# Buffer reuse, the order of one projection, early products and piecewise loads in a transformer block

## The chip, the cores and the metric

The kernel runs on one core of one Trainium2 chip. The metric is the device time of one execution in microseconds (us), as the median of several runs. One execution was also taken with the hardware profiler; all stretches below are microseconds from the start of that execution's span.

## The reference

One decoder block in float32 for 512 tokens of width 2048. A normalized input goes through one wide projection into a query latent and a key-value latent (512 each), a rotary key (64), the halves u and v of a gating unit (1024 each) and two gates (2048 each). Two branches follow, latent attention with 16 heads and a causal gating unit; their outputs are projected, gated and added, projected again by w_out and added to x. Then comes a SwiGLU feed-forward network (FFN, width 5632) and a last norm:

```python
D_MODEL, SEQ, D_FF = 2048, 512, 5632
q_lat, kv_lat, k_pe, u, v, g0, g1 = split(rms_norm(x) @ w_in)
a = mla(q_lat, kv_lat, k_pe) @ w_o_attn        # 16 heads, causal
s = (gelu(u) * (tril(w_s) @ rms_norm(gelu(v)) + b_s)) @ w_o_sgu
x = x + (sigmoid(g0) * a + sigmoid(g1) * s) @ w_out
h = rms_norm(x)
x = x + (silu(h @ w_gate) * (h @ w_up)) @ w_down
return rms_norm(x, g_final)
```

## The kernel before

**Arithmetic.** Each float32 operand is split into a high and a low part, and each matmul is done as three matmuls on the parts (`mm3`, L167 to L169). A weight chunk (`chunk`, 512 KB) is loaded by a DMA on SP's queue (L151) into a float32 buffer, cast to its high part on ACT (L152), and the low part is made by a subtraction on DVE (L153); 24 matmuls of 512 columns use it. The wide projections for u and the gates ("the x run"), and for gate and up of the FFN, go by `run` instead: each job loads 2 MB of weights (L408), makes seven sums of its quarters (L374 cast, L375 subtraction, L394 and L397 sums), and multiplies each with one of seven "forms" of the activations. One such product is 24 matmuls of 256 columns (L385 to L387), three for each of eight pairs (kp) of operand blocks. `forms_x` and `f_forms` make the forms of one kp (a cast at L331 and a subtraction at L117).

**Memory.** Nearly all of SBUF is two arenas with an allocator: `ar` (144 units of 1 KB per partition) holds split operands, `af` (52 units) holds raw float32 loads and results. `get` takes the free piece of least cost: pieces of 4 units prefer the part of `ar` from unit 112 up, then a block of eight units that is already partly in use ("packing"), and only then the piece that has been free for longest. The program's order on each engine is fixed when the program is built; a new tile waits for the last reader of the piece it is given.

**Order of stages.** The latents (w_lat) to 100 us; the v projection in two passes (g = 0, 1) of four PSUM banks each, 108 to 217 us, with 32 transposes of the latents (`latents`, L311) and the making of x's forms between its chunks; the x run to 646 us; attention and the gating unit to 957 us; w_osgu, w_oattn and w_out to 1477 us, the latter in four column blocks c with `scaled(c - 1)` (16 transposes, L810) inside the next one; the FFN's products, 1497 to 2391 us, which begin with `f_rest` (the last transposes, L810, the forms of kp 6 and 7, and `row_bcast`, L214 and L215); and the down projection to 3041 us. In the down projection, `down` multiplies eight hidden tiles (four kp) with four column blocks of w_down, five times over, 80 chunks in all; the next eight tiles are loaded on POOL's queue (L159) and split (L135 on ACT, L136 on DVE) by `hidden` before it. Four last hidden tiles have their weights prepared apart (L926). PE's order follows the code.

Of the kernel before, what the change touches and what calls it, by code (L numbers as in the profile page):

```python
# [9 lines left out]
F32 = mybir.dt.float32  # L10
# [35 lines left out]
class Arena:  # L46

    def __init__(self, tile, units, keep, large):  # L50
        self.tile, self.keep, self.large, self.clock = tile, keep, large, 0
        self.free_at = [0] * units
        self.held = {}

    def get(self, n, low=False):
        best = None
        end = (self.keep if n >= self.large else 0) or len(self.free_at)
        for i in range(0, end - n + 1, n):
            span = self.free_at[i:i + n]
            if None not in span:  # L60
                block = self.free_at[i // 8 * 8:i // 8 * 8 + 8]
                cost = (i,) if low else (n < self.large and i < self.keep, n < 8 and None not in block, max(span), -i)
                if best is None or cost < best[0]:
                    best = cost, i
# [22 lines left out]
def tile_block(ctx: ExitStack, tc, a):  # L87
# [3 lines left out]
    sml = ctx.enter_context(tc.tile_pool(name="sml", bufs=8))  # L91
    psp = ctx.enter_context(tc.tile_pool(name="psp", bufs=8, space=bass.MemoryType.PSUM))
    drm = ctx.enter_context(tc.tile_pool(name="drm", bufs=1, space=bass.MemoryType.DRAM))
    ar = Arena(cst.tile([P, NR * 256], F32R, name="ar"), NR, NX, 14)
    af = Arena(cst.tile([P, NF * 256], F32, name="af"), NF, 0, 16)

    def T():
        return af.get(2)
# [143 lines left out]
        return ss  # L242


    lat = []
    lacc = cst.tile([P, 2 * NB], F32, name="lacc")

    def lat_out(g, banks):
        row = []
        for tb, ps in enumerate(banks):  # L250
            z = T()
            nc.scalar.activation(junk, ps, AF.Square, scale=rx[:, tb:tb + 1],
                                 accum_out=lacc[:, g * NB + tb:g * NB + tb + 1])
            nc.vector.tensor_scalar(out=z, in0=ps, scalar1=rx[:, tb:tb + 1], scalar2=None, op0=ALU.mult)
            row.append(z)
        lat.append(row)

    lbanks = [[PS() for _ in range(NB)] for _ in range(2)]
    for g in range(2):
        for kp in range(8):  # L260
# [7 lines left out]
    rx = rsqrt(total(xacc, NB, "xs"), D, NB, "rx")  # L268
    lat_out(0, lbanks[0])
    lat_out(1, lbanks[1])  # L270
    rl = rsqrt(lacc, R, 2 * NB, "rl")


    raw = af.get(4)
# [19 lines left out]
        nc.vector.tensor_tensor(out=kp0[own], in0=kps[own], in1=kp0[own], op=ALU.add)  # L294
    nc.vector.tensor_tensor(out=kp0, in0=kp0, in1=rxb, op=ALU.mult)
    store(kped, kp0)
    for g in range(2):
        for tb in range(NB):
            nc.vector.tensor_scalar(out=lat[g][tb], in0=lat[g][tb], scalar1=rl[:, g * NB + tb:g * NB + tb + 1],
                                    scalar2=None, op0=ALU.mult)  # L300


    latd = drm.tile([8, P, 512], F32, name="latd")
    vvd = drm.tile([2, NB, P, 512], F32, name="vvd")
    vacc = cst.tile([P, 2 * NB], F32, name="vacc")

    def latents(g):
        for k in range(4):
            ps = PS()
            for tb in range(NB):  # L310
                nc.tensor.transpose(out=ps[:, tb * P:(tb + 1) * P], in_=lat[g][tb][:, k * P:(k + 1) * P],  # L311
                                    identity=ident)
            v = (V_Q, V_KV)[g] + k
            t = T()
            nc.scalar.activation(t, ps, AF.Copy, scale=vec[:, v:v + 1])
            store(latd[g * 4 + k], t)
        drop(lat[g])

    fx = []

    def forms_x(f, fx):
# [24 lines left out]
        drop(raw)  # L346
        forms_x(f, fx)

    af.keep = 32
    for g in range(2):  # L350
        banks = [PS() for _ in range(NB)]
        for kp in range(8):
            gemm_tm(banks, a["w_v"][g, kp], kp, aT, kp == 0, kp == 7)
            if g == 0 and kp in (2, 4):
                latents(kp // 2 - 1)
            if g == 0 and kp in (3, 5, 7):
                x_forms(kp // 2 - 1)
            if g == 1:
                drop(aT[kp * 2:kp * 2 + 2])
                if kp in (1, 3, 5):  # L360
                    x_forms(kp // 2 + 3)
        for tb, ps in enumerate(banks):
            t = T()
            nc.scalar.activation(t, ps, AF.Gelu_apprx_tanh, scale=rx[:, tb:tb + 1])
# [12 lines left out]

    FORM = (0, 5, 6, 4, 1, 2, 3)

    def product(ps, w, xs, first):  # L380
        hi, lo = w
        for kp, x in enumerate(xs):
# [5 lines left out]
        drop(w)  # L388

    def bank():  # L390
        return PS()[:, :256]
# [10 lines left out]
    class Unit:  # L402
# [32 lines left out]
            drop(self.raw)  # L435
            return w

        def multiply(self, i, w, fx):
            if i == 0:
# [3 lines left out]
            product(self.banks[(0, 1, 2, 1, 0, 1, 2)[i]], w, xs, i < 3)  # L443

        def read(self, i):
            ba, bb, bd = self.banks
# [20 lines left out]
    def run(jobs, fx, rest, ends, lead=3):  # L467


        jobs = list(jobs)  # L470
        last = 7 * len(jobs) - 7
        units, ready = {}, {}

        def unit(n):
            if n < len(jobs):
                units[n] = Unit(*jobs[n])

        unit(0)
        for g in range(last + 7 + lead + 1):
            g1, g2 = g - lead, g - lead - 1  # L480
            if g2 >= 0:
                units[g2 // 7].read(g2 % 7)
            if g < last + 7:
                ready[g] = units[g // 7].weights(g % 7)
                if g % 7 == 6:
                    unit(g // 7 + 2)
            if g == lead - 1:
                rest()
                unit(1)
            if 0 <= g1 < last + 7:  # L490
# [37 lines left out]
        x_forms(7)  # L528

    latT = []  # L530

    def latents_in(g):
        latT.append([move(load(latd[g * 4 + k])) for k in range(4)])

    run(x_jobs(), fx, x_rest, {2: lambda: latents_in(0), 4: lambda: latents_in(1)})
    qnT, kvT = latT
    af.keep = 0


    post = T()  # L540
# [283 lines left out]
    order = {(1, 3): 0, (1, 5): 1, (2, 3): 2, (3, 1): 3, (3, 3): 4, (3, 5): 5}  # L824
    for c in range(4):
        if c == 2:
            af.keep = 32
# [63 lines left out]
    run(ffn_jobs(), ff, f_rest, {2: lambda: hid.extend(hidden(0, 4)), 4: lambda: hid.extend(hidden(4, 4))})  # L891


    af.keep = 0
    for tb in range(NB):
        for c in range(4):
            h[tb][c] = load(hd[tb, :, c * 512:(c + 1) * 512])
# [2 lines left out]
        nc.vector.scalar_tensor_tensor(out=h[tb][c], in0=ps, scalar=rest[:, tb:tb + 1], in1=h[tb][c], op0=ALU.mult,  # L900
                                       op1=ALU.add)

    def down(k0, hid):
        for c in range(4):
            banks = [PS() for _ in range(NB)]
            n = len(hid) // 2
# [6 lines left out]
    k0 = 0  # L913
    while k0 < 40:
        nxt = hidden(k0 + 8, 8 if k0 < 32 else 4)
        down(k0, hid)
        k0 += 8
        hid = nxt


    wd = []
# [115 lines left out]
```

## Time and profile before

| | before |
|---|---|
| median of 3 runs | 3056.25 us (3053.21 to 3058.05) |
| profiled execution | 3052.1 us, span 3050.3 us |
| PE busy | 2761.0 us (91% of the span) |
| DVE busy | 1742.5 us (57%) |
| ACT busy | 1102.3 us (36%) |
| mean granted TensorE clock | 0.956 of full speed |
| DMA | 363.13 MB, mean 119 GB/s |

PE is TensorE, and "granted clock" is the share of full speed that the chip gave it; a stretch is at 1.00 (2.4 GHz) or 0.50 (1.2 GHz), and a value between is a mean over both. A busy time of PE near the length of a stretch says that PE sets its pace there; where it is well below, something else does.

### The profile page before, as it was taken

How to read it: one execution, taken by the hardware profiler on the slowest of the kernel's cores; microseconds unless marked ns; L12 is line 12 of the kernel's file. 1: busy time of each engine (PE TensorE's matmuls, PEld its weight loads, DVE VectorE, ACT ScalarE, POOL GpSimd, SP SyncE). 2: the span in 40 equal slices, each digit the busy share in tenths (PEclk: the TensorE clock that was granted, in tenths of full speed). 3: DMA queues.
4: the chain of work that ended last, by engine and by line, in shares of the span. 5: the costliest groups of instructions: out<-in, count | busy, mean ns of one | idle time of the engine just before them, and what ended most of it. 6: DMA issues, size and time to landing. Idle time of an engine off the chain costs nothing.

```text
span 3050.3 us, 41608 instructions
## 1 busy us (share of the span) xinstructions
PE 2761.0 (91%) x17320; PEld 2481.5 (81%) x17320; DVE 1742.5 (57%) x2194; ACT 1102.3 (36%) x1541; POOL 197.4 (6%) x369
## 2 busy tenths in 40 slices
PE   8888999988997789998799999999999697797896
PEld 7778999977886568887699999999999575575665
DVE  4357777776664334333688778787887332333334
ACT  5244444444563222233434444444434211211113
POOL 1000000011001210000000000000000100000000
PEclk9998999999999899999899999999999798898997
DMA  6332333343223544324233233333333422222223
GB/s 255 121 132 107 135 123 127 139 132 123 99 80 114 162 156 145 125 86 130 96 125 125 102 120 121 122 112 111 125 125 126 130 85 95 90 90 93 87 85 109
DMA packets 103900, 363.13 MB, mean 119 GB/s; under 512 B 14176, under 2 KB 14176, under 8 KB 103712
## 3 DMA queue, kind: packets, MB, share of 16 engines
q1 hardware_dynamic: 72720, 260.60, 24.4%
q0 software_dynamic: 29552, 97.28, 9.4%
q8 instruction: 135, 2.21, 0.3%
q10 hardware_dynamic: 1440, 2.60, 0.2%
q14 instruction: 53, 0.43, 0.0%
HBM read 315.07 MB, written 45.35 MB: 118 GB/s over the span
## 4 chain that ended last, share of the span: by engine, by line
PE 49%; DMA 8%; issue 5%; DVE 3%; ACT 3%; POOL 0%; ACTq 0%; POOLq 0%; SPq 0%; DVEq 0%
PE b L385 9%; PE b L386 9%; PE b L387 9%; PE b L167 8%; PE b L169 7%; PE b L168 7%; DMA af<-in_w_down 5%; DVE ar L153 2%; DMA af<-hidd 2%; ACT ar L152 2%; DMA af<-in_w_out 1%; POOL af L159 0%; ACT ar L135 0%; DVE ar L136 0%; ACT ar L331 0%
## 5 line engine op out<-in xcount | busy, mean ns | idle before, releaser
L385 PE MATMUL b<-ar 128*128 128x256 f32 x3584 | 1018.6, 284 | 20.3 <-ACT ar L331 11.5
L387 PE MATMUL b<-ar 128*128 128x256 f32 x3584 | 1017.6, 284 | 2.5 <-DVE ar L117 2.5
L386 PE MATMUL b<-ar 128*128 128x256 f32 x3584 | 1017.5, 284 | 0.0
L167 PE MATMUL b<-ar 128*128 128x512 f32 (+1 forms) x2016 | 796.2, 395 | 235.6 <-ACT ar L152 147.0
L168 PE MATMUL b<-ar 128*128 128x512 f32 (+1 forms) x2016 | 782.9, 388 | 0.0
L169 PE MATMUL b<-ar 128*128 128x512 f32 (+1 forms) x2016 | 761.9, 389 | 3.8 <-DVE ar L153 2.8
L385 PEld LDWEIGHTS b<-ar 128*128 128x128 f32 x3584 | 691.5, 193 | 21.7 <-ACT ar L331 12.1
L387 PEld LDWEIGHTS b<-ar 128*128 128x128 f32 x3584 | 691.4, 193 | 3.1 <-DVE ar L117 3.1
L386 PEld LDWEIGHTS b<-ar 128*128 128x128 f32 x3584 | 691.6, 193 | 0.0
L375 DVE TENSOR_TENSOR ar<-af,ar 128x1024 fp32r<-128x1024 f32 x448 | 544.4, 1223 | 251.3 <-ACT ar L374 249.8
L167 PEld LDWEIGHTS b<-ar 128*128 128x128 f32 x2016 | 391.1, 194 | 344.9 <-ACT ar L152 168.6
L374 ACT CAST ar<-af 128x1024 fp32r<-128x1024 f32 x448 | 459.5, 1046 | 480.7 <-DVE af L397 371.6
L153 DVE TENSOR_TENSOR ar<-af,ar 128x1024 fp32r<-128x1024 f32 (+1 forms) x224 | 268.5, 1204 | 593.8 <-ACT ar L152 581.7
L152 ACT CAST ar<-af 128x1024 fp32r<-128x1024 f32 (+1 forms) x224 | 230.6, 1034 | 721.9 <-DMA af<-in_w_down 368.0
L169 PEld LDWEIGHTS b<-ar 128*128 128x128 f32 x2016 | 390.0, 193 | 94.2 <-DVE ar L153 17.8
L168 PEld LDWEIGHTS b<-ar 128*128 128x128 f32 x2016 | 391.8, 194 | 70.5
L397 DVE TENSOR_TENSOR af<-af 128x1024 f32<-128x1024 f32 x192 | 234.6, 1222 | 4.2
L394 DVE TENSOR_TENSOR af<-b,af 128x256 f32<-128x256 f32 x320 | 134.5, 420 | 23.5 <-PE b L387 20.6
L136 DVE TENSOR_TENSOR ar<-af,ar 128x512 fp32r<-128x512 f32 x108 | 72.3, 690 | 126.5 <-ACT ar L135 116.9
L135 ACT CAST ar<-af 128x512 fp32r<-128x512 f32 x108 | 65.4, 619 | 208.9 <-DMA af<-hidd 70.0
L400 ACT COPY af<-b 128x256 f32<-128x256 f32 x128 | 47.4, 370 | 170.6 <-PE b L387 138.2
L900 DVE SCALAR_TENSOR_TENSOR af<-b,rest,af 128x512 f32<-128x512 f32 x96 | 72.0, 750 | 61.0 <-PE b L169 61.0
(214 smaller groups left out, 1185.3 us busy)
## 6 DMA issues: line engine op xcount, KB each, us to landing
af<-in_w_gate SPq DMA_DIRECT2D x88, 512.0 KB, 4.9
af<-in_w_up SPq DMA_DIRECT2D x88, 512.0 KB, 5.2
af<-in_w_down SPq DMA_DIRECT2D x88, 512.0 KB, 3.3
af<-in_w_g SPq DMA_DIRECT2D x64, 512.0 KB, 5.3
af<-in_w_oattn SPq DMA_DIRECT2D x32, 512.0 KB, 3.3
af<-in_w_out SPq DMA_DIRECT2D x32, 512.0 KB, 3.4
hidd<-af POOLq DMA_DIRECT2D x44, 256.0 KB, 2.6
af<-hidd POOLq DMA_DIRECT2D x44, 256.0 KB, 3.0
```

Of the source, the lines that this page charges most:

```text
L152: nc.scalar.copy(hi[:, :n], raw[:, :n])
L153: nc.vector.tensor_tensor(out=lo[:, :n], in0=raw[:, :n], in1=hi[:, :n].bitcast(F32), op=ALU.subtract)
L167: nc.tensor.matmul(ps, sl, mh, start=first, stop=False)
L168: nc.tensor.matmul(ps, sh, mh, start=False, stop=False)
L169: nc.tensor.matmul(ps, sh, ml, start=False, stop=last)
L374: pin(nc.scalar.copy(hv, src))
L375: pin(nc.vector.tensor_tensor(out=lv, in0=src, in1=hv.bitcast(F32), op=ALU.subtract))
L385: pin(nc.tensor.matmul(ps, lo[:, ks], xh, start=first and kp == 0, stop=False, skip_group_check=True))
L386: pin(nc.tensor.matmul(ps, hi[:, ks], xh, start=False, stop=False, skip_group_check=True))
L387: pin(nc.tensor.matmul(ps, hi[:, ks], xl, start=False, stop=kp == 7, skip_group_check=True))
L394: pin(nc.vector.tensor_tensor(out=out, in0=in0, in1=in1, op=ALU.add))
L397: pin(nc.vector.tensor_tensor(out=out, in0=in0, in1=in1, op=ALU.subtract))
```

## The change

Four things change together. (1) The allocator packs pieces only while `run` and w_out are at work, where large pieces are needed; elsewhere it takes the piece free for longest. (2) v is computed in one pass over kp with both halves g inside it, in all eight PSUM banks. The latents leave that stage: they are stored token by token, and loaded, transposed and split inside the last job of the x run. Six of x's eight forms are made within the v pass. (3) In both uses of `run`, the first three products are multiplied on the operand pairs whose forms exist (six of eight) before `rest()`, and on the others after it. (4) In the down projection the next eight hidden tiles are loaded and split two at a time, one pair for each column block, and the tiles in use are given back pair by pair in the last block.

```diff
     def get(self, n, low=False):
-        end = (self.keep if n >= self.large else 0) or len(self.free_at)
+        end = self.zone if n >= self.large else len(self.free_at)
...
-                cost = (i,) if low else (n < self.large and i < self.keep, n < 8 and None not in block, max(span), -i)
+                cost = (i,) if low else (n < self.large and i < self.keep, n < 8 and self.pack and None not in block,
+                                         max(span), -i)
...
-    ar = Arena(cst.tile([P, NR * 256], F32R, name="ar"), NR, NX, 14)
-    af = Arena(cst.tile([P, NF * 256], F32, name="af"), NF, 0, 16)
+    ar = Arena(cst.tile([P, NR * 256], F32R, name="ar"), NR, NX, 14, NX)
+    af = Arena(cst.tile([P, NF * 256], F32, name="af"), NF, 32, 16, 0)
...
-    af.keep = 32
-    for g in range(2):
-        banks = [PS() for _ in range(NB)]
-        for kp in range(8):
-            gemm_tm(banks, a["w_v"][g, kp], kp, aT, kp == 0, kp == 7)
-            if g == 0 and kp in (2, 4):
-                latents(kp // 2 - 1)
-            if g == 0 and kp in (3, 5, 7):
-                x_forms(kp // 2 - 1)
...
+    banks = [[PS() for _ in range(NB)] for _ in range(2)]
+    for kp in range(8):
+        for g in range(2):
+            gemm_tm(banks[g], a["w_v"][g, kp], kp, aT, kp == 0, kp == 7)
+        drop(aT[kp * 2:kp * 2 + 2])
+        if kp in (0, 1, 2, 3, 4, 6):
+            x_forms(len(fx))
+        if kp == 4:
+            af.keep = 16
...
     def run(jobs, fx, rest, ends, lead=3):
+        af.keep, af.pack = 32, True
...
             if g == lead - 1:
+                early = len(fx)
+                for i in range(lead):
+                    units[0].multiply(i, ready[i], fx, range(early))
                 rest()
                 unit(1)
...
-                units[g1 // 7].multiply(g1 % 7, ready.pop(g1), fx)
+                units[g1 // 7].multiply(g1 % 7, ready[g1], fx, range(early if g1 < lead else 0, len(fx)))
+                drop(ready.pop(g1))
...
+        af.keep, af.pack = 0, False
...
-    run(x_jobs(), fx, x_rest, {2: lambda: latents_in(0), 4: lambda: latents_in(1)})
+    run(x_jobs(), fx, x_rest, {2: lambda: latT.append(latents(0)), 4: lambda: latT.append(latents(1))})
...
-    def down(k0, hid):
+    for k0 in range(0, 40, 8):
+        nxt, n = [], 2 if k0 < 32 else 1
         for c in range(4):
+            nxt += hidden(k0 + 8 + c * n, n)
             banks = [PS() for _ in range(NB)]
...
-            for kp in range(n):
-                gemm_tm(banks, a["w_down"][c, k0 // 2 + kp], kp, hid, kp == 0, kp == n - 1)
+            for kp in range(4):
+                gemm_tm(banks, a["w_down"][c, k0 // 2 + kp], kp, hid, kp == 0, kp == 3)
+                if c == 3:
+                    drop(hid[kp * 2:kp * 2 + 2])
...
-        drop(hid)
...
-        nxt = hidden(k0 + 8, 8 if k0 < 32 else 4)
-        down(k0, hid)
```

The issues of SP's queue at the v projection, before: loads of w_v (L151) with those of the x run's first job, w_u (L408), between them.

```order
L275 DMA af<-in_w_kpe 128x1024
L151 DMA af<-in_w_v 128x1024 x3
L408 DMA af<-in_w_u 128x1024
L151 DMA af<-in_w_v 128x1024 x2
L408 DMA af<-in_w_u 128x1024 x5
L151 DMA af<-in_w_v 128x1024
L408 DMA af<-in_w_u 128x1024 x2
L151 DMA af<-in_w_v 128x1024 x10
```

And in the changed program (L153 and L404 are now the same lines):

```order
L293 DMA af<-in_w_kpe 128x1024
L153 DMA af<-in_w_v 128x1024 x15
L404 DMA af<-in_w_u 128x1024
L153 DMA af<-in_w_v 128x1024
L404 DMA af<-in_w_u 128x1024 x15
L404 DMA af<-in_w_g 128x1024 x64
```

Fifteen of the sixteen chunks of w_v now stand ahead of the first load of w_u.

PE's order where the FFN begins, before: the last matmul of w_out, then the transposes, `row_bcast` and the first product.

```order
L169 MATMUL b<-ar 128x512
L810 MATMUL b<-con,af 128x128 x16
L215 MATMUL b<-af,con 128x128 x4
L385 MATMUL b<-ar 128x256
L386 MATMUL b<-ar 128x256
L387 MATMUL b<-ar 128x256
```

In the changed program (L382 to L384 are the product's lines, L807 the transposes, L217 `row_bcast`), at the end of the early part of the first three products:

```order
L382 MATMUL b<-ar 128x256
L383 MATMUL b<-ar 128x256
L384 MATMUL b<-ar 128x256
L807 MATMUL b<-con,af 128x128 x16
L217 MATMUL b<-af,con 128x128 x4
L382 MATMUL b<-ar 128x256
```

Three times 18 matmuls of products now stand ahead of the transposes, and their last three times 6 behind `row_bcast`.

ACT's order from the FFN's end into the down projection, before: casts of product weights (L374), of hidden tiles (L135) and of w_down (L152).

```order
L135 CAST ar<-af 128x512 x4
L374 CAST ar<-af 128x1024
L135 CAST ar<-af 128x512 x4
L400 COPY af<-b 128x256
L135 CAST ar<-af 128x512 x8
L152 CAST ar<-af 128x1024 x16
L135 CAST ar<-af 128x512 x8
L152 CAST ar<-af 128x1024 x16
```

And in the changed program (L370, L137 and L154 in their place):

```order
L137 CAST ar<-af 128x512 x4
L370 CAST ar<-af 128x1024
L137 CAST ar<-af 128x512 x4
L396 COPY af<-b 128x256
L137 CAST ar<-af 128x512 x2
L154 CAST ar<-af 128x1024 x2
L137 CAST ar<-af 128x512
L154 CAST ar<-af 128x1024
L137 CAST ar<-af 128x512
L154 CAST ar<-af 128x1024 x2
```

Ten hidden tiles instead of sixteen stand ahead of the first w_down cast, and the others go between the casts of w_down instead of eight at a time.

## Rows read from the trace of the kernel before

**Rows 1.** Stretches: busy (count) of PE, PEld, DVE, ACT, POOL; PEclk, DMA share, GB/s.

```profile
108.25:217.20 108.95, 96.35 (x419) 78.04 (x417) 46.65 (x59) 37.43 (x48) 10.91 (x21) 0.94 0.43 147
217.20:250.00 32.80, 15.04 (x74) 13.65 (x74) 21.42 (x32) 12.76 (x16) 2.04 (x4) 0.58 0.15 52
957.00:1110.00 153.00, 111.52 (x389) 84.63 (x389) 47.45 (x57) 31.21 (x39) 28.53 (x53) 0.87 0.47 155
1110.00:1342.00 232.00, 232.00 (x1023) 192.08 (x1023) 85.16 (x100) 59.88 (x71) 18.77 (x35) 1.00 0.39 124
...
1497.20:2391.20 894.00, 889.97 (x7394) 889.69 (x7393) 703.89 (x789) 365.16 (x442) 35.27 (x66) 1.00 0.33 120
2391.20:2417.50 26.30, 0.17 (x2) 0.00 (x0) 8.47 (x15) 7.37 (x12) 6.44 (x12) 0.55 0.50 162
2417.50:3008.50 591.00, 485.88 (x1970) 375.15 (x1971) 186.25 (x206) 111.13 (x129) 15.00 (x28) 0.91 0.27 90
```

**Rows 2.** Costliest groups of the page: count, busy us, mean ns.

```profile
L153 DVE TENSOR_TENSOR ar<-af,ar 128x1024 fp32r<-128x1024 f32 (+1 forms) x224 | 268.5, 1204 | 593.8 <-ACT ar L152 581.7
L152 ACT CAST ar<-af 128x1024 fp32r<-128x1024 f32 (+1 forms) x224 | 230.6, 1034 | 721.9 <-DMA af<-in_w_down 368.0
```

**Rows 3.** PE timeline at a latent transposition in the v stage.

```profile
137.37 1.91 PE L311 MATMUL b<-con,af 128*128 128x128 f32 x16
146.48 0.79 PE L167 MATMUL b<-ar 128*128 128x512 f32 x1 [7.20 <-ACT ar L152]
```

**Rows 4.** DMA issues of SP queue in the v stage (start, duration, line).

```profile
108.08 19.14 SPq L408 DMA_DIRECT2D af<-in_w_u  x5
```

**Rows 5.** ACT timeline behind the v stage's last matmul.

```profile
217.46 0.69 ACT L364 ACTIVATE af<-b,rxo 128x512 f32<-128x512 f32 x1
...
218.81 1.03 ACT L374 CAST ar<-af 128x1024 fp32r<-128x1024 f32 x1
```

**Rows 6.** PE timeline where the last column block of w_out begins.

```profile
1427.72 0.80 PE L167 MATMUL b<-ar 128*128 128x512 f32 x1 [9.74 <-ACT ar L152]
```

**Rows 7.** PE timeline between w_out and the FFN's products.

```profile
1477.25 1.12 PE L810 MATMUL b<-con,af 128*128 128x128 f32 x8
...
1493.80 1.22 PE L215 MATMUL b<-af,con 128*128 128x128 f32 x4 [13.30 <-DVE af L214]
```

**Rows 8.** DVE timeline in the same stretch.

```profile
1480.75 1.22 DVE L375 TENSOR_TENSOR ar<-af,ar 128x1024 fp32r<-128x1024 f32 x1 [1.16 <-ACT ar L374]
```

**Rows 9.** POOL loads of hidden tiles at the end of the FFN.

```profile
2407.90 1.15 POOL L159 DMA_DIRECT2D af<-hidd  x2 [3.53 <-DVE ar L136]
```

**Rows 10.** SP first issue of w_down behind them.

```profile
2413.00 52.99 SPq L151 DMA_DIRECT2D af<-in_w_down  x10
```

**Rows 11.** Waits from the first w_down matmul to the last part's weights.

```profile
ACT ar L152 <- DMA af<-in_w_down: 363.8, 73, 6.8
...
PE b L167 <- ACT ar L152: 114.7, 28, 26.1
...
ACT ar L135 <- DMA af<-hidd: 43.5, 14, 4.6
```

**Rows 12.** ACT weight casts in the down projection.

```profile
2427.68 1.05 ACT L152 CAST ar<-af 128x1024 fp32r<-128x1024 f32 x1 [4.59 <-DMA af<-in_w_down]
2433.38 1.05 ACT L152 CAST ar<-af 128x1024 fp32r<-128x1024 f32 x1 [4.64 <-DMA af<-in_w_down]
```

**Rows 13.** POOL loads of the next eight hidden tiles.

```profile
2509.85 1.06 POOL L159 DMA_DIRECT2D af<-hidd  x2 [100.80 <-DVE ar L153]
...
2523.79 1.18 POOL L159 DMA_DIRECT2D af<-hidd  x2 [3.50 <-DVE ar L136]
```

**Rows 14.** PE timeline where successive w_osgu chunks share a buffer.

```profile
1007.69 0.39 PE L169 MATMUL b<-ar 128*128 128x512 f32 x1
1010.56 0.47 PE L167 MATMUL b<-ar 128*128 128x512 f32 x1 [2.48 <-DVE ar L153]
```

**Rows 15.** ACT cast into that buffer.

```profile
1008.12 1.04 ACT L152 CAST ar<-af 128x1024 fp32r<-128x1024 f32 x1 [8.68 <-PE b L169]
```

More of the change, by code (lines that the diff above doesn't have):

```diff
@@ L46, with __init__ @@
 class Arena:
-    def __init__(self, tile, units, keep, large):
-        self.tile, self.keep, self.large, self.clock = tile, keep, large, 0
-        self.free_at = [0] * units
+    def __init__(self, tile, units, zone, large, keep):
+        self.tile, self.zone, self.large, self.keep, self.clock = tile, zone, large, keep, 0
+        self.free_at, self.pack = [0] * units, False
         self.held = {}
@@ L242, in total, with latents @@
         return ss
-    lat = []
+    latd = drm.tile([2, NB, P, 512], F32, name="latd")
     lacc = cst.tile([P, 2 * NB], F32, name="lacc")
+    lat = {}
     def lat_out(g, banks):
-        row = []
+        zs, acc = [], lacc[:, g * NB:(g + 1) * NB]
         for tb, ps in enumerate(banks):
             z = T()
-            nc.scalar.activation(junk, ps, AF.Square, scale=rx[:, tb:tb + 1],
-                                 accum_out=lacc[:, g * NB + tb:g * NB + tb + 1])
+            nc.scalar.activation(junk, ps, AF.Square, scale=rx[:, tb:tb + 1], accum_out=acc[:, tb:tb + 1])
             nc.vector.tensor_scalar(out=z, in0=ps, scalar1=rx[:, tb:tb + 1], scalar2=None, op0=ALU.mult)
-            row.append(z)
-        lat.append(row)
+            zs.append(z)
+        rl = rsqrt(acc, R, NB, "rl%d" % g)
+        for tb, z in enumerate(zs):
+            nc.vector.tensor_scalar(out=z, in0=z, scalar1=rl[:, tb:tb + 1], scalar2=None, op0=ALU.mult)
+            store(latd[g, tb], z)
+    def latents(g):
+        zs, rows = [load(latd[g, tb]) for tb in range(NB)], []
+        for k in range(4):
+            ps = PS()
+            for tb in range(NB):
+                nc.tensor.transpose(out=ps[:, tb * P:(tb + 1) * P], in_=zs[tb][:, k * P:(k + 1) * P], identity=ident)
+            v = (V_Q, V_KV)[g] + k
+            rows.append(split(ps, vec[:, v:v + 1]))
+        drop(zs)
+        return rows
     lbanks = [[PS() for _ in range(NB)] for _ in range(2)]
@@ L267, in tile_block @@
                 x_stats(kp - 4)
-    rx = rsqrt(total(xacc, NB, "xs"), D, NB, "rx")
-    lat_out(0, lbanks[0])
+            if g == 1 and kp == 1:
+                rx = rsqrt(total(xacc, NB, "xs"), D, NB, "rx")
+                lat_out(0, lbanks[0])
     lat_out(1, lbanks[1])
-    rl = rsqrt(lacc, R, 2 * NB, "rl")
     raw = af.get(4)
@@ L296, in tile_block @@
     store(kped, kp0)
-    for g in range(2):
[L298 to L303, printed above, removed]
     vvd = drm.tile([2, NB, P, 512], F32, name="vvd")
     vacc = cst.tile([P, 2 * NB], F32, name="vacc")
[L307 to L317, printed above, removed]
     fx = []
@@ L347, in x_forms @@
         forms_x(f, fx)
-    af.keep = 32
-    for g in range(2):
-        banks = [PS() for _ in range(NB)]
-        for kp in range(8):
-            gemm_tm(banks, a["w_v"][g, kp], kp, aT, kp == 0, kp == 7)
-            if g == 0 and kp in (2, 4):
-                latents(kp // 2 - 1)
-            if g == 0 and kp in (3, 5, 7):
-                x_forms(kp // 2 - 1)
[L358 to L362, printed above, removed]
+    banks = [[PS() for _ in range(NB)] for _ in range(2)]
[7 more added lines that the diff above has]
+            af.keep = 16
+    for tb in range(NB):
+        for g in range(2):
             t = T()
-            nc.scalar.activation(t, ps, AF.Gelu_apprx_tanh, scale=rx[:, tb:tb + 1])
+            nc.scalar.activation(t, banks[g][tb], AF.Gelu_apprx_tanh, scale=rx[:, tb:tb + 1])
             nc.scalar.activation(junk, t, AF.Square, accum_out=vacc[:, tb * 2 + g:tb * 2 + g + 1])
@@ L378, in tile_block, with product @@
     FORM = (0, 5, 6, 4, 1, 2, 3)
-    def product(ps, w, xs, first):
+    def product(ps, w, xs, kps, first):
         hi, lo = w
-        for kp, x in enumerate(xs):
+        for kp in kps:
+            x = xs[kp]
             ks = slice(kp * P, (kp + 1) * P)
@@ L387, in product @@
             pin(nc.tensor.matmul(ps, hi[:, ks], xl, start=False, stop=kp == 7, skip_group_check=True))
-        drop(w)
     def bank():
@@ L436, in weights, with multiply @@
             return w
-        def multiply(self, i, w, fx):
-            if i == 0:
+        def multiply(self, i, w, fx, kps):
+            if i == 0 and 0 in kps:
                 self.banks = [bank() for _ in range(3)]
@@ L442, in multiply @@
             xs = [f[n] if isinstance(f, list) else f[:, n * 512:(n + 1) * 512] for f in fx]
-            product(self.banks[(0, 1, 2, 1, 0, 1, 2)[i]], w, xs, i < 3)
+            product(self.banks[(0, 1, 2, 1, 0, 1, 2)[i]], w, xs, kps, i < 3)
         def read(self, i):
@@ L530, in tile_block @@
     latT = []
-    def latents_in(g):
-        latT.append([move(load(latd[g * 4 + k])) for k in range(4)])
-    run(x_jobs(), fx, x_rest, {2: lambda: latents_in(0), 4: lambda: latents_in(1)})
+    run(x_jobs(), fx, x_rest, {2: lambda: latT.append(latents(0)), 4: lambda: latT.append(latents(1))})
     qnT, kvT = latT
-    af.keep = 0
     post = T()
@@ L826, in tile_block @@
         if c == 2:
-            af.keep = 32
+            af.keep = 16
+        af.pack = True
         ht = [load(a["x"][tb * P:(tb + 1) * P, c * 512:(c + 1) * 512]) for tb in range(NB)]
@@ L901, in more @@
                                        op1=ALU.add)
-    def down(k0, hid):
+    for k0 in range(0, 40, 8):
+        nxt, n = [], 2 if k0 < 32 else 1
         for c in range(4):
+            nxt += hidden(k0 + 8 + c * n, n)
             banks = [PS() for _ in range(NB)]
-            n = len(hid) // 2
-            for kp in range(n):
-                gemm_tm(banks, a["w_down"][c, k0 // 2 + kp], kp, hid, kp == 0, kp == n - 1)
+            for kp in range(4):
+                gemm_tm(banks, a["w_down"][c, k0 // 2 + kp], kp, hid, kp == 0, kp == 3)
+                if c == 3:
+                    drop(hid[kp * 2:kp * 2 + 2])
             for tb, ps in enumerate(banks):
                 more(tb, c, ps)
-        drop(hid)
-    k0 = 0
-    while k0 < 40:
-        nxt = hidden(k0 + 8, 8 if k0 < 32 else 4)
-        down(k0, hid)
-        k0 += 8
         hid = nxt
+    k0 = 40
     wd = []
```

1 line of the change is left out of this document (removed).

## The prediction

> **What bounds the kernel now.** The page's first part gives PE 91% of the span, so I read the stretches next, to see where the other 9% lies [rows 1]. From 1110 to 1342 us PE never stops: 232.00 us for 1023 matmuls of 512 columns is 0.2268 us each at clock 1.00, so a chunk of 24 takes 5.44 us. The FFN's products are as full: 894.00 us for 7394 is 0.121 us each, 2.9 us per product. There only fewer matmuls could help, and the change takes none away. What it can win lies in four stretches: the v projection, the start of the x run, the turn from the FFN to the down projection, and the down projection itself. Of 217.20 to 250.00 us PE is busy 15.04 at clock 0.58. Of the turn, 26.30 us are idle but for 0.17. The down projection up to its last part takes 591.00 us for 80 chunks and 48 matmuls more, 1968 in all, whose own time is 446.3; it loses 144.7 us. Then the waits of each stretch say which of them ends last.
>
> The profiled execution took 3052.1 us, 1.8 more than its span, and lies 4.2 below the median of the runs. I make the sum against 3052.1 and take about half of that difference back at the end.
>
> **v in one pass.** The 384 matmuls need 87.1 us and their stretch is 108.95, so 21.9 are lost. In it are the 32 latent transposes (1.91 us for 16) and one wait of 7.2 us for a cast [rows 3], which waited for a load of w_v held up on SP's queue: five loads of w_u ahead of it hold the queue for 19.14 us [rows 4]. In the new order fifteen w_v loads go first, the transposes are gone, and four weight buffers rotate. I find no wait that ends late and take all 21.9 (bounds 15 and 21.9).
>
> The transposes come back in the x run's last job: 3.8 us, plus up to 3 if the two groups of latents, which are now loaded by POOL just ahead, are late. Cost 5 (3.8 to 7).
>
> The x run's first three products, 72 matmuls, end 32.7 us behind the v pass, where they need 8.7. Now 54 of them can go before the forms of kp 6 and 7. But one gelu and square takes 1.35 us on ACT [rows 5], eight are now due at the end of the pass and the first weight cast stands behind them: about 1.4 us later than before. And the other 18 matmuls still wait for the last two forms, which go through the same DVE queue. I put the end at 28.6 behind the pass: gain 4 (0 to 15). Together v and x: 21.9 - 5 + 4 = 21.
>
> Keeping all eight banks in one pass is what the Trainium skill's page "Perfetto Trace Analysis", section "Matmuls", speaks against: independent groups should rotate through banks so that one's evacuation lies beside the next one's matmuls. By the rows, half of the evacuation still lies beside the pass's last chunk, since 5.44 us hold four steps of 1.35; were all eight steps to come behind it, the price would be 5.4 more and this term 16.
>
> **Longest-free pieces elsewhere.** In attention and w_oattn the buffers that the built program assigns are as far apart as before; 0 (-5 to 5). In w_osgu the high part still goes into one piece chunk after chunk, as before, so the clock of 0.87 there stays [rows 1].
>
> **w_out.** The last column block begins after 9.74 us idle, its first matmul at half speed (0.80 us) [rows 6]; with the clock about 11.6. Its first raw buffers are now free early, and this goes. But the raw buffer of its fourth chunk now waits for the transposes of `scaled(2)`, which stand three matmul groups ahead on PE. A load, cast (1.03 us) and subtraction (1.20) [rows 2] in a row take 5.7 us [rows 12], and the clock falls again: 7.5. Gain 4 (0 to 11).
>
> **Early products in the FFN.** Between the transposes at 1477.25 and `row_bcast` PE idles 13.3 us [rows 7]. The weights of the first product are ready at 1481.97 [rows 8], so 54 matmuls at half speed (0.21 us each, 11.5 us) fit in. They cost nothing only because PE idles there; but the transposes, which began at 1477.25, now stand behind them, at about 1494, and all that makes forms 6 and 7 and the broadcast is queued behind these on ACT and DVE. The last 18 matmuls then end near 1505, where the 72 ended near 1507. Gain 2 (-6 to 6).
>
> **The turn to the down projection.** POOL loads hidden tiles in pairs, the last at 2407.90 [rows 9], and SP issues the first w_down load at 2413.00 [rows 10], because both use one piece of `af`. Ten tiles instead of sixteen now stand ahead of the first w_down cast. Three pairs fewer at 4.65 us, from four pairs between 2509.85 and 2523.79 [rows 13], are 14; the load no longer has to wait for the last pair, some 4 more. Gain 18 (12 to 22).
>
> **The down projection.** Before, one raw buffer serves all chunks: ACT waits 363.8 us for loads [rows 11], and casts follow at 5.7 us [rows 12], more than the 5.44 that PE needs. And each block of eight tiles is a stop: POOL waits 100.80 us for its buffer, then issues four pairs one after another while w_down is shut out [rows 13]. PE's own part in this is 114.7 us [rows 11]. Now four raw buffers rotate; load, cast and subtraction fit four times over, and both losses go.
>
> A new one comes. Hidden tiles lie above unit 112 of `ar`, where small pieces prefer to be. In the last column block each pair is dropped after its kp, which frees just the eight units that the next chunk wants. So the next chunk's high and low part go into the piece that PE has only just read, and so on until tiles take it again. By the pieces assigned, 14 of the 80 chunks stand directly behind the last reader of their piece, and 10 more with 7 to 10 other matmuls between. The rows show this wait in w_osgu: the last reader starts at 1007.69, the cast at 1008.12 [rows 15], the next chunk at 1010.56 [rows 14], 2.87 us. In w_down the high part's last reader stands one matmul from the end and the low part's first reader is third, so four matmuls (0.9) lie between: 1.96 us lost each, 27; the other ten lose 0.15 to 0.8, 5. To these I add DVE's four evacuations ahead of some subtractions, 5; hidden casts that wait on ACT with weight casts behind them, 10, between 0 and today's 43.5 [rows 11]; the last four tiles' weights, 8; and the clock.
>
> The clock: in the w_osgu stretch it averages 0.87 over 153 us, so some 40 us are at half speed; over 16 such gaps that costs at most 1.25 us each [rows 1]. For 24 gaps that is 30 at most, but those gaps here come in two halves; I take 8. The Trainium skill's page "TensorE: Matmul & The Clock Gate", section "HAM oscillation", lets only long idle gaps lower the clock, which would make it 0 and the sum 8 less; the 0.87 behind gaps of 2.87 us speaks against it.
>
> Loss after: 27 + 5 + 5 + 10 + 8 + 8 = 63, where it was 144.7: gain 82, call it 85 with small waits of today's chain that I have not listed (bounds 30 and 130).
>
> **Sum.** 21 + 0 + 4 + 2 + 18 + 85 = 130, so 3052.1 - 130 = 2922, and toward the median 2925.
>
> **Rivals.** (a) The reused pieces cost next to nothing, since weights of a later chunk are prepared ahead: the loss falls to about 20, 43 less: 2880. For it: the ten with other work between. Against it: w_osgu. (b) They cost as in w_osgu throughout, 2.87 + 1.25 for 24 chunks, 99 in place of 45, and x's and FFN's starts win nothing: 2985. (c) Loads set the pace: with four raw buffers w_down loads run beside each other and each takes longer; the chunk stays at 5.7 us, 21 more over 80 chunks: 2946. Against it: the first cast gap of 5.7 holds load, cast and subtraction in a row, so the load alone is near 3.4, below 5.44. (d) The other side: reuse spreads beyond the chunks that I count. Each such chunk costs up to 4.1 us; with 45 won elsewhere and 144.7 to give back, 46 of 80 chunks make it slower; all 80 give 3052 - 45 - 145 + 330 = 3192. Against it: the built program assigns 24.
>
> **Chances and range.** The forecast 0.60, (a) 0.15, (b) 0.13, (c) 0.08, (d) 0.03, no change 0.01. The likeliest gives 2925, with 2900 to 2955 of its own; the range for eight in ten reaches to (a) and (b), 2880 to 2985. About 0.2% (6 us) is what a measurement can tell from no change: faster 0.96, same 0.015, slower 0.025.
>
> **What would show it.** After: v's 384 matmuls end near 195 us without a gap over 1 us; no idle of 10 us in w_out but one near 6 behind the third transposes; the FFN's transposes start behind products; the turn takes about 8 us; ACT's wait for in_w_down falls under 60 us and its wait for PE rises; gaps of 1 to 2 us stand in fours to eights near the ends of hidden blocks. It would be wrong if hidden loads still stop PE for over 10 us, if the reused pieces lower the clock each time, or if DVE is late with x's last forms.

## The result and the profile after

The changed kernel takes 2864.66 us (median of 4 runs, 2863.98 to 2865.96), before 3055.09 us in the same comparison: a ratio of 0.9376 (0.936 to 0.9393). That is 6% faster, outside the forecast range of 2880 to 2985 on the fast side. The profiled span fell from 3050.3 to 2863.3 us, by 187.0, where the sum said 130.

Stage by stage in the two PE timelines (us). The first row counts from the span's start, each other from the row above to the start of the matmul that it names:

| stage | before | after | gain | forecast |
|---|---|---|---|---|
| v ends at | 217.03 | 194.83 | 22.2 | 21.9 |
| v's end to the x run's last product | 428.6 | 431.8 | -3.2 | -1 |
| to w_out's last matmul | 831.4 | 801.3 | 30.1 | 4 |
| to the FFN's last product | 914.1 | 913.8 | 0.2 | 2 |
| to the first w_down matmul | 26.4 | 8.4 | 18.0 | 18 |
| to the last w_down matmul | 623.2 | 503.5 | 119.7 | 85 |

The last column has the terms of the sum, with v and x taken apart. The stretches that answer to [rows 1], in the trace after:

```profile
108.24:195.00 86.76, 86.76 (x384) 71.70 (x382) 45.04 (x59) 31.75 (x35) 6.47 (x12) 1.00 0.49 169
195.00:224.50 29.50, 15.17 (x76) 13.95 (x76) 21.05 (x31) 13.45 (x20) 2.17 (x4) 0.73 0.17 57
...
906.00:1070.00 164.00, 125.59 (x492) 99.21 (x492) 53.79 (x80) 39.03 (x64) 30.14 (x56) 0.88 0.50 160
1070.00:1302.00 232.00, 232.00 (x1029) 192.18 (x1028) 86.38 (x101) 61.61 (x73) 18.79 (x35) 1.00 0.40 131
...
1454.00:2342.10 888.10, 883.30 (x7326) 882.54 (x7325) 702.23 (x788) 364.90 (x444) 35.68 (x67) 0.99 0.33 120
2342.10:2350.20 8.10, 0.00 (x0) 0.00 (x0) 3.97 (x9) 2.50 (x4) 2.56 (x6) 0.71 0.92 323
```

v is a full stretch at clock 1.00. In the turn to the down projection PE is idle for 8.1 us. The gating stage keeps its clock of 0.88. The two weight preparations on the page, with what the engine waited for last [rows 2]:

```profile
L155 DVE TENSOR_TENSOR ar<-af,ar 128x1024 fp32r<-128x1024 f32 (+1 forms) x224 | 267.7, 1204 | 420.8 <-ACT ar L154 414.1
L154 ACT CAST ar<-af 128x1024 fp32r<-128x1024 f32 (+1 forms) x224 | 229.8, 1035 | 663.5 <-PE b L171 354.0
```

The casts are as long as before. Most of ACT's idle time ahead of them now ends with a matmul that had read the buffer, not with a load of w_down: buffers, not loads, set their time. In the waits from 2280 to 2860 us that answers to [rows 11]:

```profile
ACT ar L154 <- PE b L171: 174.9, 9, 49.1
...
ACT ar L154 <- DMA af<-in_w_down: 74.8, 31, 5.9
...
PE b L169 <- ACT ar L154: 22.6, 19, 8.1
```

PE's wait for casts is 22.6 us, from 114.7. Both hold the turn (8.1 and 26.1), so in the down projection itself it is 14.5, from 88.6; the prediction took the 114.7 for the down projection alone. ACT's wait for w_down's loads fell from 363.8 to 74.8 us, and not below 60, as the prediction expected. PE's waits that are left stand at the reused pieces of `ar`, as in this piece of PE's timeline, with ACT's cast and DVE's subtraction of the same chunk below it:

```profile
2429.86 0.39 PE L171 MATMUL b<-ar 128*128 128x512 f32 x1
2431.16 0.50 PE L169 MATMUL b<-ar 128*128 128x512 f32 x1 [0.91 <-ACT ar L154]
2431.50 0.39 PE L170 MATMUL b<-ar 128*128 128x512 f32 x1
2431.73 0.40 PE L169 MATMUL b<-ar 128*128 128x512 f32 x1
2431.97 0.39 PE L170 MATMUL b<-ar 128*128 128x512 f32 x1
2432.20 0.40 PE L169 MATMUL b<-ar 128*128 128x512 f32 x1
2432.43 0.39 PE L170 MATMUL b<-ar 128*128 128x512 f32 x1
2432.66 0.39 PE L171 MATMUL b<-ar 128*128 128x512 f32 x1
```

```profile
2430.07 1.04 ACT L154 CAST ar<-af 128x1024 fp32r<-128x1024 f32 x1 [5.64 <-PE b L170]
```

```profile
2431.14 1.22 DVE L155 TENSOR_TENSOR ar<-af,ar 128x1024 fp32r<-128x1024 f32 x1 [5.46 <-ACT ar L154]
```

The high part's last reader is L170, one before the end, so the cast starts at 2430.07 and PE goes on at 2431.16. The built program then puts three pairs of L169 and L170, which use the high part, ahead of the first L171, which needs the low part: the subtraction from 2431.14 to 2432.36 lies beside six matmuls. PE's order does not follow the code here. The code has the three lines in turn, as PE runs them in an earlier chunk that does not wait:

```profile
2419.78 0.39 PE L169 MATMUL b<-ar 128*128 128x512 f32 x1
2420.01 0.39 PE L170 MATMUL b<-ar 128*128 128x512 f32 x1
2420.23 0.39 PE L171 MATMUL b<-ar 128*128 128x512 f32 x1
```

From 2429.86 to 2431.16 are 1.30 us, 1.1 more than a matmul's own spacing, where I had 1.96.

### The profile page after: what moved, and what is told of

The parts are those of the page before. It is cut to its first block, busy times and chain, and to the rows that moved or that the text cites. A ratio compares the mean times of both kernels' runs of the same rounds, so it can differ in the third digit from the quotient of the medians.

```text
span 2863.3 us, 41568 instructions
## 1 busy us (share of the span) xinstructions
PE 2725.3 (95%) x17320; PEld 2479.6 (87%) x17320; DVE 1739.3 (61%) x2200; ACT 1094.0 (38%) x1534; POOL 197.3 (7%) x369
## 3 DMA queue, kind: packets, MB, share of 16 engines
q1 hardware_dynamic: 72720, 260.60, 26.1%
## 5 line engine op out<-in xcount | busy, mean ns | idle before, releaser
L382 PE MATMUL b<-ar 128*128 128x256 f32 x3584 | 1021.9, 285 | 23.9 <-DVE ar L371 14.6
L384 PE MATMUL b<-ar 128*128 128x256 f32 x3584 | 1020.9, 285 | 3.4 <-DVE ar L119 3.4
L169 PE MATMUL b<-ar 128*128 128x512 f32 (+1 forms) x2016 | 780.8, 388 | 95.9 <-DVE ar L155 51.0
L170 PE MATMUL b<-ar 128*128 128x512 f32 (+1 forms) x2016 | 773.8, 384 | 0.0
L171 PE MATMUL b<-ar 128*128 128x512 f32 (+1 forms) x2016 | 762.5, 383 | 0.1
L382 PEld LDWEIGHTS b<-ar 128*128 128x128 f32 x3584 | 694.5, 194 | 26.3 <-DVE ar L371 9.0
L384 PEld LDWEIGHTS b<-ar 128*128 128x128 f32 x3584 | 694.4, 194 | 4.1 <-DVE ar L119 4.1
L370 ACT CAST ar<-af 128x1024 fp32r<-128x1024 f32 x448 | 459.3, 1046 | 481.6 <-DVE af L393 367.8
L169 PEld LDWEIGHTS b<-ar 128*128 128x128 f32 x2016 | 386.0, 191 | 186.7 <-ACT ar L154 48.5
L154 ACT CAST ar<-af 128x1024 fp32r<-128x1024 f32 (+1 forms) x224 | 229.8, 1035 | 663.5 <-PE b L171 354.0
L171 PEld LDWEIGHTS b<-ar 128*128 128x128 f32 x2016 | 385.6, 191 | 75.8 <-DVE ar L155 2.4
L170 PEld LDWEIGHTS b<-ar 128*128 128x128 f32 x2016 | 386.2, 192 | 70.1
L138 DVE TENSOR_TENSOR ar<-af,ar 128x512 fp32r<-128x512 f32 x100 | 66.4, 688 | 74.7 <-ACT ar L137 74.7
L137 ACT CAST ar<-af 128x512 fp32r<-128x512 f32 x100 | 59.6, 619 | 133.1 <-DMA af<-hidd 46.0
```

What stands on the lines that cost most here:

```text
L154: nc.scalar.copy(hi[:, :n], raw[:, :n])
L169: nc.tensor.matmul(ps, sl, mh, start=first, stop=False)
L170: nc.tensor.matmul(ps, sh, mh, start=False, stop=False)
L171: nc.tensor.matmul(ps, sh, ml, start=False, stop=last)
L370: pin(nc.scalar.copy(hv, src))
```

## The experiments

A ratio is to the kernel before, run on the same chip. "The stretch of 1901 matmuls" runs from the first w_down matmul to the 1901st.

**e1_pack: part 1 undone alone.**

```diff
-                cost = (i,) if low else (n < self.large and i < self.keep, n < 8 and self.pack and None not in block,
+                cost = (i,) if low else (n < self.large and i < self.keep, n < 8 and None not in block,
```

> The changed kernel with packing everywhere (part 1 undone alone). Theory A, part 1 gives the gains I did not forecast: the attention and gating stage gets back its 22 us (wait of 8 us for the first w_uq load among them), and the down projection goes back to one raw buffer, 0.6 us per chunk over 80 chunks, 50 us; about 2865 + 75 = 2940. Theory B, those gains come from the new order of the other parts and packing matters little: 2865 to 2885.

Measured: 3079.03 us, ratio 1.0082 (1.0064 to 1.0101): 0.8% slower than the kernel before. Both theories were too low; A's direction holds and its size does not. The new order of v, the x run, the FFN and the down projection with packing wins nothing in all. v still ends early, at 195.37 us, but from the first w_down matmul to the 1901st is 619.6 us, where the kernel before took 548.7 and the changed one 455.6. In that stretch, from 2371 to 2990 us:

```profile
POOL af L161 <- DVE ar L155: 577.1, 19, 34.4
...
ACT ar L154 <- DMA af<-in_w_down: 267.1, 56, 6.7
...
PE b L169 <- ACT ar L154: 133.0, 50, 10.7
```

With packing, hidden tiles and w_down share one piece of `af`: each pair's load takes w_down's only raw buffer, and PE stops for about 4 to 7 us some twenty times, where it stopped three times for 19 and once for 10 in the kernel before.

**e9_before_lru: the kernel before with part 1 alone.** `self.pack` is added to the cost as in the change and set for v, `run` and w_out; so v still packs here, which it does not in the change.

```diff
-... n < 8 and None not in block, max(span), -i)
+... n < 8 and self.pack and None not in block, max(span), -i)
```

> The kernel before with part 1 alone: no packing outside the two uses of run, v and w_out. Theory A: 3055 - 75 = about 2980, with the stops of 19 us before each block of eight hidden tiles still there, unless these too came from the packed raw buffer, then about 2915. Theory B: 3035 to 3055.

Measured: 2863.03 us, ratio 0.9379 (0.9365 to 0.9393), as much as the whole change gains and more than theory A said. v ends at 216.39, as before; from the x run's last product to w_out's end it takes 800.2 us (changed: 801.3); and the stretch from the first w_down matmul to the 1901st is full:

```profile
2370.80:2803.50 432.70, 432.66 (x1901) 357.62 (x1902) 179.51 (x199) 107.26 (x124) 17.20 (x33) 1.00 0.38 124
```

Hidden tiles are still loaded eight ahead, but POOL's pairs now come one behind each chunk, 5.4 us apart, and nothing is shut out:

```profile
2484.20 1.07 POOL L159 DMA_DIRECT2D af<-hidd  x2 [64.22 <-DVE ar L153]
2489.64 1.07 POOL L159 DMA_DIRECT2D af<-hidd  x2 [4.37 <-DVE ar L153]
```

**e10_before_ar: the same for `ar` alone.** The attribute is set to `units == NF`, so that `af` packs and `ar` does not.

> The kernel before, with packing off in the arena of split operands (ar) alone and kept in that of raw loads (af). Theory J, the single raw buffer of w_down, the stops of 19 us and the late w_uq load all come from af: 3040 to 3055, no gain. Rival K, packed split operands carry part of it: 2950 to 3020.

Measured: 3053.6 us, ratio 1.0003 (0.9993 to 1.0014). That is theory J: packing in `ar` carries nothing by itself, so part 1's gain needs `af` free of packing. `af` alone was not run.

**e5_one_raw: every raw load of w_down into one piece of `af`.**

```diff
-        raw, hi, lo = af.get(4), ar.get(4), ar.get(4)
+        raw, hi, lo = af.get(4, low), ar.get(4), ar.get(4)
```

Here and in e4_one_split `low`, which asks for the lowest free piece, is set for the down projection's 80 chunks alone.

> The changed kernel with every raw load of w_down forced into one piece of af. Theory A, the single raw buffer was worth 50 us before (486.7 us for 1926 matmuls of 436.8): 2865 + 45 = 2910, casts 5.7 us apart waiting for loads. Rival: the chunks that wait for their split piece already hide part of it: 2885.

Measured: 2929.18 us, ratio 0.9589 (0.9571 to 0.9606), 64 above the changed kernel: more than either. The stretch of 1901 matmuls takes 518.40 us in place of 455.60.

**e4_one_split: every w_down chunk's split parts into one piece of `ar`.**

```diff
-        raw, hi, lo = af.get(4), ar.get(4), ar.get(4)
+        raw, hi, lo = af.get(4), ar.get(4, low), ar.get(4, low)
```

> The changed kernel with every w_down chunk's split parts forced into one piece of ar, so that all 80 chunks wait for their predecessor's last reader. Theory C, a reused piece costs about 1.2 us because PE reads the high part first and the low part a few matmuls later, and leaves the clock at full speed: 56 more such chunks, 2865 + 67 = about 2932. Rival D, the price of my sum (1.96 us each and some clock): 2865 + 110 to 180 = 2975 to 3045.

Measured: 2945.33 us, ratio 0.9651 (0.9636 to 0.9665), 81 above the changed kernel over the 56 more chunks that I count: 1.4 each. That is between the theories and nearer to C, with the clock up as C has it:

```profile
2343.50:2883.70 540.20, 462.14 (x1901) 355.72 (x1902) 179.57 (x195) 103.40 (x119) 17.23 (x32) 0.98 0.31 99
```

**e2_eight and e3_drop_end: the down projection of before, and the piecewise one that gives tiles back at the block's end.**

```diff
-            nxt += hidden(k0 + 8 + c * n, n)
...
-                if c == 3:
-                    drop(hid[kp * 2:kp * 2 + 2])
+        drop(hid)
```

The first line is taken out in e2_eight alone, which loads all eight ahead of the block.

> The changed kernel with its down projection as before (eight hidden tiles loaded ahead, all given back at the block's end), packing off. Theory E, the allocator alone removed the stops and the single raw buffer, and piecewise loading only adds reused pieces: the 23 us that the down projection of the kernel before with part 1 was shorter come here too, 2865 - 23 = 2842. Rival F, piecewise loading carries part of the gain when v and the x run are in the new form: 2865 to 2900.

> The changed kernel with hidden tiles still loaded in pairs, but given back only at the end of each block. Theory E: the reused pieces come from giving back pair by pair, so their 23 us go, 2842. Rival G: the pairs' casts between the weight casts cost it, 2865.

Measured: 2842.03 us (0.9313, 0.9299 to 0.9327) and 2844.82 us (0.9325, 0.9311 to 0.9339). Theory E in both, within 3 us. Giving tiles back pair by pair costs about 20 us: the stretch of 1901 matmuls takes 455.6 us in the changed kernel, 439.9 in e3_drop_end. Loading in pairs neither costs nor gains in all: in e2_eight the stretch is 433.0, but the FFN and the turn take 5.0 longer than in e3_drop_end.

**e6_no_early: part 3 undone.**

```diff
-                early = len(fx)
-                for i in range(lead):
-                    units[0].multiply(i, ready[i], fx, range(early))
+                early = 0
```

> The changed kernel without early products (part 3 undone in both uses). Theory: the 72 matmuls of the first three products end 5 us later in the x run and 3 us later in the FFN, but most of it is given back behind them at a clock that rises sooner: 2865 to 2870. Rival: they are worth the idle time that they fill, 2875 to 2885.

Measured: 2865.42 us, ratio 0.9396 (0.9382 to 0.941), as the changed kernel. The 72 matmuls end 32.8 us behind v's end in place of 28.0, and in the FFN 30.2 behind w_out's last matmul in place of 26.8, but the last products come only 0.7 and 0.9 us later. Two stretches of each trace show how the lead goes, first e6_no_early:

```profile
196.00:229.00 33.00, 14.53 (x75) 12.94 (x74) 21.44 (x31) 14.70 (x21) 2.17 (x4) 0.64 0.16 54
229.00:260.00 31.00, 31.00 (x260) 31.00 (x260) 23.70 (x25) 14.30 (x17) 1.09 (x2) 1.00 0.40 153
```

and the changed kernel, with 18 matmuls more by 33 us, but 14 by 64 us, since its clock rises later:

```profile
194.80:228.00 33.20, 18.87 (x93) 17.45 (x92) 23.37 (x33) 15.64 (x22) 2.17 (x4) 0.71 0.15 54
228.00:259.00 31.00, 31.00 (x256) 31.00 (x255) 23.36 (x26) 14.17 (x17) 1.09 (x2) 0.98 0.42 153
```

The rest of the lead is lost behind these; which product gives it back was not followed.

**e7_two_pass: v in two passes of four banks, the rest as changed.**

```diff
...
-    for kp in range(8):
-        for g in range(2):
-            gemm_tm(banks[g], a["w_v"][g, kp], kp, aT, kp == 0, kp == 7)
...
+    for g in range(2):
+        banks = [PS() for _ in range(NB)]
+        for kp in range(8):
+            gemm_tm(banks, a["w_v"][g, kp], kp, aT, kp == 0, kp == 7)
...
```

The lines left out make six forms between the chunks of the two passes.

> The changed kernel with v in two passes of four banks as before, but the latents in the x run and six forms in the v passes as changed. Theory H, the 22 us of the v stage come from the order of its loads on SP's queue and from the transposes' removal, not from the eight-bank pass: v ends near 195 us, 2865. Rival I, the one pass itself brings them, since it frees the input tiles kp by kp and so the room for forms and loads: v ends near 205 to 216, 2875 to 2887.

Measured: 2862.84 us, ratio 0.9378 (0.9364 to 0.9392); v ends at 195.51. Theory H: the eight-bank pass brings nothing. The first product starts 4.1 us behind v's end as before, in place of 5.9 in the one pass.

**e8_hi_first: the order of the three matmuls in w_osgu and w_oattn.**

```diff
+    def mm3h(ps, sh, sl, mh, ml, first, last):
+        nc.tensor.matmul(ps, sh, mh, start=first, stop=False)
+        nc.tensor.matmul(ps, sh, ml, start=False, stop=False)
+        nc.tensor.matmul(ps, sl, mh, start=False, stop=last)
...
-                mm3(ps, hi[:, k, ms], lo[:, k, ms], xh, xl, first and k == 0, last and k == 3)
+                mm3h(ps, hi[:, k, ms], lo[:, k, ms], xh, xl, first and k == 0, last and k == 3)
```

The call stands in `gemm_fm`, which only these two projections use; `mm3` stays as it was for the others.

> The changed kernel with the three matmuls of w_osgu and w_oattn in the order high-high, high-low, low-high. Theory C, what a reused piece costs depends on which part PE reads first: in w_osgu it needs the low part first, so cast and subtraction lie in a row (2.8 us a gap); with the high part first the subtraction lies beside matmuls, and 14 gaps shrink to about 1.4 us and below what lowers the clock: 2865 - 20 to 35 = 2830 to 2845. Rival: the next chunk waits for the same cast and the same clock, 2855 to 2865.

Measured: 2836.11 us, ratio 0.9288 (0.9273 to 0.9304), 29 less. The gaps of 2.78 us in the changed kernel, first pair of rows, are now mostly 1.30, as in w_down, second pair:

```profile
935.88 0.39 PE L171 MATMUL b<-ar 128*128 128x512 f32 x1
938.66 0.50 PE L169 MATMUL b<-ar 128*128 128x512 f32 x1 [2.40 <-DVE ar L155]
```

```profile
945.70 0.39 PE L171 MATMUL b<-ar 128*128 128x512 f32 x1
946.99 0.50 PE L169 MATMUL b<-ar 128*128 128x512 f32 x1 [0.91 <-ACT ar L154]
```

The stage's clock is 0.95 from 930 to 1040 us. It is 1.00 behind six gaps of 1.30, and falls only in the middle, where PE has gaps of 3.88, 2.41 and 2.37 us:

```profile
930.00:980.70 50.70, 44.87 (x191) 33.66 (x190) 14.63 (x18) 7.52 (x9) 9.36 (x18) 1.00 0.55 189
980.70:1020.00 39.30, 29.10 (x100) 20.97 (x99) 16.48 (x22) 13.10 (x19) 10.75 (x20) 0.87 0.52 172
1020.00:1040.00 20.00, 17.50 (x71) 12.57 (x69) 6.45 (x9) 3.90 (x5) 4.33 (x8) 1.00 0.59 197
```

**e11_best and e12_keep: the two edits together, and then `ar` free of its preference.** e11_best is e2_eight with e8_hi_first. e12_keep adds:

```diff
     qnT, kvT = latT
+    ar.keep = 0
...
+    ar.keep = NX
     oT = [move(load(ogd[k]), low=True) for k in range(KD)]
```

> The changed kernel with the down projection as before and the high part first in w_osgu and w_oattn. The 23 us and the 28 us lie in stages apart and add: 2865 - 51 = 2814. Rival: they overlap or start a new wait, 2825 to 2836.

> As the kernel before it in this call, and small pieces of ar may also lie below unit 112 from the x run's end to w_osgu's end. Theory L, it is the preference for units from 112 up that puts every w_osgu chunk's high part into one piece; without it the remaining gaps of 1.3 us and their clock go, 14 x 1.1 + some 15 us of other small waits in attention: 2785 to 2800. Rival M, ar is simply full there: 2814.

Measured: 2817.94 us (0.9226, 0.9211 to 0.924) and 2769.84 us (0.9071, 0.9056 to 0.9086). The first adds up within its spread. The second beats theory L by 15 us: `ar` had room, and it was the preference for units from 112 up that put each chunk's high part into the piece just read. The stage is now full, at full speed:

```profile
885.00:1005.00 120.00, 120.00 (x568) 101.00 (x567) 56.07 (x83) 42.25 (x68) 31.12 (x58) 1.00 0.69 231
```

Of the 48 us between the two, about 16 lie ahead of the last attention transposes, as theory L had it, and 33 behind them, where it had 15. This is the fastest version here, 95 us below the changed kernel.

## Why the forecast was wrong

**Where it failed: the down projection and "longest-free pieces elsewhere".** The sum had 85 and 0 for these; they measured 119.7, and 22.0 up to the end of w_osgu. I put part 1's effect down to raw buffers for w_down and saw no other place for it, and I priced the reused pieces that part 4 makes at 45 us. The runs show that part 1 alone gains as much as the whole change: 2863.03 us with it alone, 3079.03 with all but it. That the first is so near 2864.66 is a cancellation. With parts 1 to 3 (e2_eight) it is 2842.03: parts 2 and 3 win 21 us on top of part 1, nearly all in v (which ends at 216.39 in e9_before_lru and at 195.89 in e2_eight), and part 4 loses 23 again.

- **The 19 us stops.** I had them removed by loading in pairs. e9_before_lru keeps eight at a time and has none; e1_pack loads in pairs and has 20 smaller ones. What mattered was that loads of w_down and hidden tiles no longer share a piece. The forecast of 18 for the turn was right by luck: e9_before_lru, which loads eight tiles ahead, also turns in 10.9 us, so part 1 alone brings 15.5 of it.
- **A reused piece.** The term was 32 for 24 chunks, with 5 for evacuations and 8 for the clock. The stretch of 1901 matmuls took 455.6 us for 431.1 of its own (1901 x 0.2268), so all its losses, the clock's included, are 24.5, at most 1.0 per chunk where the sum had 1.9. I read the piece rightly as directly reused and the order of PE wrongly: six matmuls hide the subtraction. e4_one_split's 1.4 per chunk is nearer to this than to my 1.96, and e2_eight, at 433.0 us, loses next to nothing without the reused pieces.
- **The clock.** Its 8 us did not come. Behind gaps of 1.3 to 1.8 us it stays up, as in the down projection once it has risen (first row), and behind 2.78 it falls, as in the gating stage (second row):

```profile
2355.80:2805.80 450.00, 435.28 (x1890) 352.33 (x1889) 171.62 (x191) 99.87 (x114) 17.73 (x33) 1.00 0.35 113
930.00:1066.00 136.00, 97.59 (x344) 74.74 (x343) 39.32 (x47) 26.00 (x32) 24.67 (x46) 0.86 0.47 149
```

The Trainium skill's page "TensorE: Matmul & The Clock Gate", section "HAM oscillation", lets only long idle gaps lower the clock. For the short gaps this trace agrees with it; the 0.86 behind gaps that are mostly 2.78 to 2.88 us does not.

- **Hidden casts on ACT (10) and the last weights (8)** cost little or nothing: the 24.5 us hold all that the casts can have cost, and from the 1901st w_down matmul to the last one takes 47.9 us, all busy, where it took 74.5. With part 1 alone it is 47.8, so packing had made this loss too.
- **Attention.** Of 22.0 us, 8.0 come ahead of the first attention transposes. Before, PE waited 7.57 us for the first weights behind the x run:

```profile
653.46 0.80 PE L167 MATMUL b<-ar 128*128 128x512 f32 x1 [7.57 <-DVE ar L153]
```

ACT's first cast of them waited for a load of w_uq; of the loads issued by then, two at 638.38 and one at 646.07, the row doesn't say which:

```profile
651.59 0.83 ACT L152 CAST ar<-af 128x768 fp32r<-128x768 f32 x1 [2.25 <-DMA af<-in_w_uq]
```

In the changed kernel the loads are issued from 613.71 on, and the first two casts are made ahead of the run's last product at 626.65, so that PE goes straight on:

```profile
622.51 1.60 ACT L154 CAST ar<-af 128x768 fp32r<-128x768 f32 x2
```

This wait is gone without part 1 too: e1_pack, which packs everywhere, issues the first of these loads as early (first row) and has no such wait. With part 1 alone 3.22 us of it stay (second row):

```profile
612.07 3.24 SPq L153 DMA_DIRECT2D af<-in_w_uq  x2
```

```profile
648.07 0.79 PE L167 MATMUL b<-ar 128*128 128x512 f32 x1 [3.22 <-DVE ar L153]
```

e6_no_early and e2_eight, without parts 3 and 4, do not have it either, which leaves part 2. The remaining 14 us lie in many waits under 4 us and in two more w_osgu chunks done among the heads. The chunks do go with part 1: behind the last attention transposes 1392 matmuls are left up to w_out's first transposes in e9_before_lru and in the changed kernel, 1434 in e1_pack and before. Which buffer gave each wait was not tried. I had looked at the distance of reuse in `ar`, where it is as before, and not at when loads may start.

**What held.** v (21.9 forecast, 22.2 measured), by the order of the loads or the transposes' removal, as I had it, and not by the single pass (e7_two_pass). Which of the two stays open; the transposes' own time is 3.8 us of it. The transposes came back at 3.8 us and 2.1 of waiting. In w_out the idle 10 us are gone and the new wait behind `scaled(2)` came, 4.58 us for a forecast of 5.7, so 8.1 gained in place of 4:

```profile
1391.83 1.91 PE L807 MATMUL b<-con,af 128*128 128x128 f32 x16
1398.33 0.80 PE L169 MATMUL b<-ar 128*128 128x512 f32 x1 [4.58 <-ACT ar L154]
```

In the FFN the early products fill PE's idle time and push the transposes to 1443.22, 15 us behind w_out; the 72 matmuls end 3 us earlier and the stage 0.2, where I had 2.

```profile
1443.22 1.91 PE L807 MATMUL b<-con,af 128*128 128x128 f32 x16
```

Of the rivals, (a) came nearest. Its loss of about 20 us in the down projection is close to the 24.5 measured, though for another reason than it gave, and it too had nothing for the stages from attention to w_osgu. Behind the eight-bank pass the first product is 1.8 us later than behind two passes of four banks, and the time is the same. The Trainium skill's page "Perfetto Trace Analysis", section "Matmuls", has independent groups rotate through banks, so that the evacuation of one lies beside the next one's matmuls. Here that is worth these 1.8 us at the pass's end and nothing in the total.

## What to carry to other kernels

An allocator that reuses the piece freed last turns a deep buffer into a single one without a word in the code that uses it; look for casts that wait for loads at the full period of load, cast and subtraction, and test the allocator alone before reordering. What a reused buffer costs depends on which of its readers comes first: put the operand that is ready first in front, and the rest of the preparation lies beside matmuls. When several edits are made at once, undo each alone and do each alone: here one of four gains as much as all together, because the 21 us that a second wins a third loses again.

## What the runs showed of the hardware

In the same kind of work the granted clock fell behind gaps of 2.78 us between the starts of two matmuls, and not behind gaps of 1.30 us: it averaged 0.86 from 930 to 1066 us of the changed kernel, with 11 gaps of 2.78 to 2.88 us and three of 3.5 to 4.9, and was 1.00 from 930 to 980.7 us of e8_hi_first, with six gaps of 1.30. DMA carried 231 GB/s beside a full PE in e12_keep's gating stage, where the changed kernel had 149; loads at that rate did not hold PE up there.
